# Expert token lists by 8-byte indirect transfers through DRAM, in place of one-hot matmuls

## The chip, the cores and the metric

The kernel runs on one core of a Trainium2 chip. The metric is the device time of one execution in microseconds (us), as the median of several runs. Before the change it is 3347.19 us (three runs, 3345.39 to 3347.9).

## What is computed

One layer of a diffusion backbone over 2048 tokens of width 1024: a mixer (convolution heads and neighbourhood attention), then expert-choice routed SwiGLU experts, then a final RMSNorm. The change lies in the experts. The reference, cut to them:

```python
def ec_moe(h, w_router, w_gate, w_up, w_down):
    B, T, _ = h.shape
    cap = EC_FACTOR * T // N_EXPERTS             # 2 * 2048 // 16 = 256
    aff = jax.nn.softmax((h @ w_router).astype(jnp.float32), axis=-1)
    wts, tok = lax.top_k(jnp.swapaxes(aff, 1, 2), cap)
    bidx = jnp.arange(B)[:, None, None]
    xs = h[bidx, tok]
    hid = jax.nn.silu(jnp.einsum('becd,edf->becf', xs, w_gate)) * jnp.einsum('becd,edf->becf', xs, w_up)
    y = jnp.einsum('becf,efd->becd', hid, w_down) * wts[..., None].astype(h.dtype)
    return jnp.zeros_like(h).at[bidx, tok].add(y)
```

Each of the 16 experts takes the 256 tokens that like it best. It needs their numbers (to gather their rows and to add the results back) and their weights.

## The kernel before, in words

The program runs in stages: input projection, convolution and attention, output projection with the router, routing, experts. The expert stage (`moe`, from L1140) takes the last two thirds of the time.

**Routing** (`route`, L1083). For every token and expert it leaves in `slot` (128 partitions x 16 token blocks x 16 experts) the token's place in the expert's list, 1 to 256, or 0 if the expert did not take it. `lg` holds the affinities. `vals` holds, per token and expert, five bf16 numbers: the block number, the partition, and the affinity in three pieces.

**The token list of an expert** (`prep`, L1168). For each of the 16 token blocks VectorE (DVE) compares a row 1 to 256 with the block's `slot` column, which gives a one-hot matrix `oh` (L1171). TensorE (PE) multiplies the 16 one-hot blocks, in two halves of 128 places, with `vals` (L1177 to L1178): 32 matmuls of 5 columns per expert. DVE turns the five sums into the token number `idx` and the weight `wt` (L1180 to L1185). Two indirect transfers on GpSimd's (POOL's) queue then gather the tokens' rows from DRAM into `xr` (L1191).

**The chunks.** An expert has 24 chunks in a list (L1208): 16 of gate/up (`gate_up`, L1228: 32 matmuls, 16 of 512 columns and 16 of 256) and 8 of down (`down`, L1255: 24 matmuls of 512 columns). For each chunk `load` (L1213) brings 1 MB of weights into `raw` (3 buffers) over SyncE's (SP's) queue; ScalarE (ACT) casts it to `whi` and DVE subtracts to give `wlo` (L207, L208; 3 buffers each). In the loop over chunks (L1379) the load of chunk i+2 is issued before the work of chunk i.

**What else is in the loop.** `prep(e+1)` is called at gate/up chunk 8 of expert e (L1384); `gather(e+1, part)` (L1195), which transposes the gathered rows on PE and splits them, at down chunks 1 to 4 of expert e; `finish(e)` (L1357) at its last chunk: DVE scales the result into `y` and POOL adds it to `acc` in DRAM with two indirect transfers (L1365). The last two experts take other paths (`rows_of`, `finish_late`, `last_part`, `final`).

**What sets the order.** The framework's scheduler orders each engine's instructions: among those that its own plan takes to be ready, the one written first goes first. So work written later is put into an engine's idle places as soon as the plan has its inputs. Within `tc.manual_schedule(engines=ENG)` (L1372, `ENG` is POOL) POOL's instructions keep the order in which they are written; the region ends at chunk `REG`, 3 before the change (L1397). `self.order(a, b)` (L201) puts a behind b on its engine; `PIN` uses it for the first one-hot block of expert 2. An engine runs its instructions in that order: one that waits holds up all behind it.

The lines that matter most:

```python
            for i, (s, e, f) in enumerate(chunks):
                if i:
                    load(i + 2)
                if s == "gu":
                    gate_up(i)
                    if f == PF and e + 1 < NE:
                        prep(e + 1)
```

Of the kernel before, what the change touches and what calls it, by code (L numbers as in the profile page):

```python
# [10 lines left out]
F32 = mybir.dt.float32  # L11
F32R = mybir.dt.float32r
BF16 = mybir.dt.bfloat16
F16 = mybir.dt.float16
I32 = mybir.dt.int32
AF = mybir.ActivationFunctionType
OP = mybir.AluOpType
# [3 lines left out]
P = 128  # L21
D = 1024
KT = D // P
T = 2048
NT = T // P
# [9 lines left out]
E = 16  # L35
NE = E
F = 2048
CAP = 256
# [7 lines left out]
CTX0 = ("q", 0)  # L46
ALL = {mybir.EngineType.DVE, mybir.EngineType.PE, mybir.EngineType.Activation, mybir.EngineType.Pool, mybir.EngineType.SP}
MAIN = {mybir.EngineType.DVE, mybir.EngineType.PE, mybir.EngineType.Activation}
REG = 3
PIN = (2,)  # L50
ENG = {mybir.EngineType.Pool}
LAT = 0.8
LEAD = 2.2
# [70 lines left out]
class Net:  # L124
# [1015 lines left out]
    def moe(self):  # L1140
        nc, tc, A, S = self.nc, self.tc, self.A, self.S
        with ExitStack() as es:
            pool = es.enter_context(tc.tile_pool(name="p6", bufs=1, reuse_waits="tile"))
            ps = es.enter_context(tc.tile_pool(name="ps6", bufs=1, space=PSUM, reuse_waits="tile"))
            g2 = pool.tile([P, D], F32, name="g2")
            X, XR, AXW = {}, {}, {}
# [19 lines left out]
                                                       op0=OP.mult, op1=OP.add)  # L1166

            def prep(e):  # L1168
                oh = pool.tile([P, NT, CAP], BF16, name="oh", bufs=1)
                for c in range(NT):  # L1170
                    m = nc.vector.tensor_scalar(oh[:, c, :], self.iob, self.slot[:, c, e:e + 1], None, op0=OP.is_equal)  # L1171
                    if e in PIN and c == 0:
                        self.order(m, self.xlo)
                pi = ps.tile([P, 2, 8], F32, name="tp6", tag="tp", bufs=1)
                for hf in range(2):
                    for c in range(NT):
                        nc.tensor.matmul(pi[:, hf, :5], oh[:, c, hf * P:(hf + 1) * P], self.vals[:, c, e, :],  # L1177
                                         start=(c == 0), stop=(c == NT - 1))  # L1178
                ax = pool.tile([P, 5, 8], F32, name="ax", bufs=2)[:, :2]
                nc.vector.tensor_copy(ax[:, :, :5], pi[:, :, :5])  # L1180
                idx = pool.tile([P, 2], I32, name="idx", bufs=3)
                wt = pool.tile([P, 2], F32, name="wt", bufs=3)
                nc.vector.scalar_tensor_tensor(idx, ax[:, :, 0], float(P), ax[:, :, 1], op0=OP.mult, op1=OP.add)
                nc.vector.tensor_add(wt, ax[:, :, 2], ax[:, :, 3])
                nc.vector.tensor_add(wt, wt, ax[:, :, 4])  # L1185
                AXW[e] = (idx, wt)
                XR[e] = []
                for i in range(2):
                    xr = pool.tile([P, D], F32, name="xr", bufs=2)
                    XR[e].append(xr)  # L1190
                    nc.gpsimd.indirect_dma_start(  # L1191
                        out=xr, out_offset=None, in_=S["h2d"][:, :],
                        in_offset=bass.IndirectOffsetOnAxis(ap=idx[:, i:i + 1], axis=0))

            def gather(e, part):  # L1195
                if part == 0:
                    X[e] = pool.tile([P, KT, 2 * CAP], F32R, name="xt6", bufs=2)
                xt = X[e]
                i, a = divmod(part, 2)
                xr = XR[e][i]  # L1200
                tp = ps.tile([P, 4, P], F32, name="tp6", tag="tp" if e else "mm", bufs=1 if e else 7)
                for k in range(4):
                    nc.tensor.transpose(tp[:, k, :], xr[:, (4 * a + k) * P:(4 * a + k + 1) * P], self.ident)
                hi = xt[:, 4 * a:4 * a + 4, i * P:(i + 1) * P]
                nc.scalar.copy(hi, tp)
                self.xlo = nc.vector.tensor_sub(xt[:, 4 * a:4 * a + 4, CAP + i * P:CAP + (i + 1) * P], tp, hi.bitcast(F32))  # L1206
# [6 lines left out]
            def load(i):  # L1213
                if i >= len(chunks):
                    return
                s, e, f = chunks[i]
                raw = pool.tile([P, 2, 1024], F32, name="raw", tag="raw", bufs=3)
                src = A["w_gu"][e, f].rearrange("p a k c -> p a (k c)") if s == "gu" else A["w_dn"][e, f]
                nc.sync.dma_start(raw, src)
                hi = pool.tile([P, 2, 1024], F32R, name="whi6", bufs=3)  # L1220
                lo = pool.tile([P, 2, 1024], F32R, name="wlo6", bufs=3)
                for a in range(2):
                    self.split(raw[:, a], hi[:, a], lo[:, a], nc.gpsimd if i < 3 else None)
                W[i] = (hi, lo)
# [3 lines left out]
            def gate_up(i):  # L1228
                s, e, f = chunks[i]
                hi, lo = [a.rearrange("p a (k c) -> p a k c", k=KT) for a in W.pop(i)]  # L1230
                xt = X[e]
                pg = []
                for a in range(2):
                    p_ = ps.tile([P, 512], F32, name="pgu", tag="mm", bufs=7)
                    for k in range(KT):
                        nc.tensor.matmul(p_, hi[:, a, k], xt[:, k, :], start=(k == 0), stop=False)  # L1236
                        nc.tensor.matmul(p_[:, :CAP], lo[:, a, k], xt[:, k, :CAP], start=False, stop=(k == KT - 1))  # L1237
                    pg.append(p_)
                t = pool.tile([P, 2, CAP], F32, name="gt6", bufs=2)
                for a in range(2):  # L1240
                    nc.scalar.copy(t[:, a], pg[a][:, CAP:])  # L1241
                    nc.vector.tensor_add(t[:, a], pg[a][:, :CAP], t[:, a])  # L1242
                sl = pool.tile([P, CAP], F32, name="sl6", bufs=2)
                nc.scalar.activation(sl, t[:, 0], AF.Silu)
                nc.vector.tensor_mul(sl, sl, t[:, 1])  # L1245
                hh = pool.tile([P, CAP], F32R, name="hh", bufs=20)
                hl = pool.tile([P, CAP], F32R, name="hl", bufs=20)
                self.split(sl, hh, hl)
                hid[e, f] = (hh, hl)
# [50 lines left out]

            def rows_of(e):
                idx = AXW[e][0]
                ga = pool.tile([P, 2, D], F32, name="ga", bufs=1)
                for a in range(2):
                    nc.gpsimd.indirect_dma_start(
                        out=ga[:, a], out_offset=None, in_=S["acc"][:, :],
                        in_offset=bass.IndirectOffsetOnAxis(ap=idx[:, a:a + 1], axis=0))
                return ga
# [48 lines left out]
            def finish(e):  # L1357
                idx, wt = AXW[e]
                for a in range(2):
                    y = pool.tile([P, D], F32, name="y6", tag="y6", bufs=2)  # L1360
                    for b in range(2):
                        sb = slice(b * 512, (b + 1) * 512)
                        nc.vector.scalar_tensor_tensor(y[:, sb], py[e][a][b], wt[:, a:a + 1], g2[:, sb],  # L1363
                                                       op0=OP.mult, op1=OP.mult)
                    nc.gpsimd.indirect_dma_start(  # L1365
                        out=S["acc"][:, :], out_offset=bass.IndirectOffsetOnAxis(ap=idx[:, a:a + 1], axis=0),
                        in_=y, in_offset=None, compute_op=OP.add)
# [8 lines left out]
            prep(0)  # L1376
            for i in range(4):
                gather(0, i)
            for i, (s, e, f) in enumerate(chunks):  # L1379
                if i:  # L1380
                    load(i + 2)
                if s == "gu":
                    gate_up(i)
                    if f == PF and e + 1 < NE:  # L1384
                        prep(e + 1)
                    if e == 0 and f in (3, 6, 9, 12, 15):
                        gate2(2 * f // 3 - 2)
                else:
                    if 0 <= f - GF < 4 and e + 1 < NE:
                        gather(e + 1, f - GF)  # L1390
                    down(i)
                    if f == 7:
                        if e < NE - 2:
                            finish(e)
                        elif e < NE - 1:
                            finish_late(e, ga)
                if i == REG:  # L1397
                    region.close()
                if e >= NE - 2:
                    if i % 24 == 1:  # L1400
                        ga = rows_of(e)
                        if e == NE - 2:
                            gf = pool.tile([P, D], F32, name="gf")
                            nc.sync.dma_start(gf, A["ngf"].to_broadcast([P, D]))
                    if i - 24 * (NE - 2) in FIN:
                        final(FIN.index(i - 24 * (NE - 2)))
# [28 lines left out]
```

## Time and profile before

| | |
|---|---|
| median of 3 runs | 3347.19 us (3345.39 to 3347.9) |
| the profiled execution, its own time | 3346.83 us |
| its span in the profile | 3345.0 us |
| mean granted clock of TensorE | 0.986 |
| PE, DVE, ACT, POOL busy | 97%, 70%, 50%, 12% of the span |
| mean transfer rate | 190 GB/s |

The times of the trace count from the start of the span. The profile's rows name the line of the code, the engine, and the operation as output <- inputs. PEld is PE's loading of weights, which overlaps its matmuls. The expert stage starts near 1130 us; expert e from 1 to 13 starts near 1282 + 137 (e - 1). A row of a timeline may merge several instructions of one kind (x10); its duration then runs from the first one's start to the last one's end.

### The profile page before, as it was taken

The page shows a single profiled execution, that of the slowest core. Times are in us where ns is not written, and L with a number is a line of the kernel's source. Part 1 is how long each engine was busy: PE and PEld are TensorE (multiplying, and loading weights), DVE is VectorE, ACT ScalarE, POOL GpSimd, SP SyncE. Part 2 cuts the span into 40 slices and gives each one's busy share as a digit, 9 for nine tenths or more (in the row PEclk, how much of TensorE's full clock was granted, in tenths as well). Part 3 has the DMA queues.
Part 4 walks back from the last instruction along what each step waited for, and adds up shares of the span by engine and source line. Part 5 has one row for each costly group of instructions (what it writes and reads, how often), then busy time and mean ns, then how long its engine had stood idle before and what let it go on. Part 6 is the DMA issues. An engine that isn't in the chain of part 4 may idle for free. (4 is left out here: it accounts for less than half of the span.)

```text
span 3345.0 us, 47917 instructions
## 1 busy us (share of the span) xinstructions
PE 3242.2 (97%) x18394; PEld 2749.2 (82%) x18394; DVE 2344.0 (70%) x3645; ACT 1660.1 (50%) x2788; POOL 414.1 (12%) x729
## 2 busy tenths in 40 slices
PE   7999999999999599999999999999999999999998
PEld 4788887899777488888888888888888888888887
DVE  6898988888666776665666756656667666665766
ACT  7211124788433255454554545545555455454654
POOL 3100002344211200000000000000000000001221
PEclk9999999999999699999999999999999999999999
DMA  6244329997432466565565565665556556556765
GB/s 234 76 139 127 110 98 249 227 224 189 146 127 107 170 220 197 201 204 198 202 208 191 206 201 191 212 201 195 196 201 207 197 201 200 195 210 208 283 251 202
DMA packets 159585, 635.61 MB, mean 190 GB/s; under 512 B 47926, under 2 KB 62678, under 8 KB 106108
## 3 DMA queue, kind: packets, MB, share of 16 engines
q1 hardware_dynamic: 138172, 542.68, 47.4%
q0 software_dynamic: 21184, 89.86, 10.9%
q8 instruction: 145, 2.38, 0.3%
q14 instruction: 84, 0.69, 0.1%
HBM read 560.38 MB, written 72.10 MB: 189 GB/s over the span
## 5 line engine op out<-in xcount | busy, mean ns | idle before, releaser
L1236 PE MATMUL pgu<-xt,whi 128*128 128x512 f32 x4096 | 1446.7, 398 | 0.5 <-DVE xt L1206 0.5
L208 DVE TENSOR_TENSOR wlo<-raw,whi 128x1024 fp32r<-128x1024 f32 x762 | 919.0, 1220 | 649.0 <-ACT whi L207 646.4
L1237 PE MATMUL pgu<-xt,wlo 128*128 128x256 f32 x4096 | 1149.8, 281 | 0.2 <-DVE wlo L208 0.2
L207 ACT CAST whi<-raw 128x1024 fp32r<-128x1024 f32 x768 | 793.1, 1050 | 565.7 <-PE py L1272 277.9
L1236 PEld LDWEIGHTS pgu<-xt,whi 128*128 128x128 f32 x4096 | 769.3, 188 | 189.8 <-DVE xt L1206 0.9
L1237 PEld LDWEIGHTS pgu<-xt,wlo 128*128 128x128 f32 x4096 | 773.7, 189 | 1.1 <-DVE wlo L208 0.5
L1268 PE MATMUL py<-whi,hh 128*128 128x512 f32 x1024 | 405.3, 396 | 0.0
L1269 PE MATMUL py<-wlo,hh 128*128 128x512 f32 x1024 | 399.8, 390 | 0.0
L1272 PE MATMUL py<-whi,hl 128*128 128x512 f32 x1024 | 316.4, 390 | 0.0
L534 DVE SCALAR_TENSOR_TENSOR cacc<-v,k,cacc 128x2048 f32<-128x2048 f32 x120 | 281.6, 2347 | 1.7
L1241 ACT COPY gt<-pgu 128x256 f32<-128x256 f32 x512 | 188.5, 368 | 177.2 <-PE pgu L1237 176.8
L471 PE MATMUL mm<-hhi,whi 128*128 128x512 f32 x576 | 227.1, 394 | 0.0
L1272 PEld LDWEIGHTS py<-whi,hl 128*128 128x128 f32 x1024 | 192.2, 188 | 41.5
L473 PE MATMUL mm<-hhi,wlo 128*128 128x512 f32 x576 | 224.5, 390 | 0.0
L1268 PEld LDWEIGHTS py<-whi,hh 128*128 128x128 f32 x1024 | 192.4, 188 | 39.0 <-issue 0.2
L472 PE MATMUL mm<-hlo,whi 128*128 128x512 f32 x576 | 224.2, 389 | 0.0
L1269 PEld LDWEIGHTS py<-wlo,hh 128*128 128x128 f32 x1024 | 192.5, 188 | 38.0 <-issue 0.2
L1242 DVE TENSOR_TENSOR gt<-pgu,gt 128x256 f32<-128x256 f32 x512 | 213.9, 418 | 6.0 <-ACT gt L1241 5.9
L207 ACT CAST hh<-sl 128x256 fp32r<-128x256 f32 x256 | 104.1, 406 | 223.2 <-DVE sl L1245 223.2
L1365 POOL DMA_INDIRECT acc<-y,idx x28 | 51.6, 1842 | 1263.8 <-DVE y L1363 1184.6
L737 DVE CUSTOM_DVE_ANT_0 pt<-sp,bi 128x640 f32<-128x640 f32 (+1 forms) x128 | 113.6, 887 | 31.0 <-PE sp L730 29.5
L208 DVE TENSOR_TENSOR hl<-sl,hh 128x256 fp32r<-128x256 f32 x256 | 108.8, 425 | 34.0 <-ACT hh L207 7.1
(317 smaller groups left out, 4122.8 us busy)
## 6 DMA issues: line engine op xcount, KB each, us to landing
raw<-w_gu SPq DMA_DIRECT2D x256, 1024.0 KB, 4.8
raw<-w_dn SPq DMA_DIRECT2D x128, 1024.0 KB, 4.8
bi<-bias SPq DMA_DIRECT2D x14, 960.0 KB, 11.0
wm<-wm POOLq DMA_DIRECT2D x24, 512.0 KB, 4.5
vb<-vd SPq DMA_DIRECT2D x119, 96.0 KB, 3.5
wraw<-w_in SPq DMA_DIRECT2D x20, 512.0 KB, 4.2
kh<-kh POOLq DMA_DIRECT2D x16, 576.0 KB, 12.5
kl<-kl POOLq DMA_DIRECT2D x16, 576.0 KB, 14.5
```

What stands on the lines that cost most here:

```text
L207: nc.scalar.copy(hi, full)
L208: (eng or nc.vector).tensor_sub(lo, full, hi.bitcast(F32))
L471: nc.tensor.matmul(ps, w[0][:, k, :], h[0][:, k, :], start=(k == 0), stop=False)
L472: nc.tensor.matmul(ps, w[0][:, k, :], h[1][:, k, :], start=False, stop=False)
L473: nc.tensor.matmul(ps, w[1][:, k, :], h[0][:, k, :], start=False, stop=(k == KT - 1))
L534: nc.vector.scalar_tensor_tensor(acc, v[:, w:w + T], cwt[:, j, w:w + 1], acc, op0=OP.mult, op1=OP.add)
L1236: nc.tensor.matmul(p_, hi[:, a, k], xt[:, k, :], start=(k == 0), stop=False)
L1237: nc.tensor.matmul(p_[:, :CAP], lo[:, a, k], xt[:, k, :CAP], start=False, stop=(k == KT - 1))
L1242: nc.vector.tensor_add(t[:, a], pg[a][:, :CAP], t[:, a])
L1268: nc.tensor.matmul(py[e][a][b], hh[:, sa], hi[:, ff, sb], start=(f == 0), stop=False)
L1269: nc.tensor.matmul(py[e][a][b], hh[:, sa], lo[:, ff, sb], start=False, stop=False)
L1272: nc.tensor.matmul(py[e][a][b], hl[:, sa], hi[:, ff, sb], start=False, stop=(f == 15))
```

## The change

For experts 2 to 15 (`NL = 2`) the one-hot matrices and their matmuls are gone; experts 0 and 1 keep them. `list_setup`, once, before the first chunk, makes on POOL and DVE two tables over all tokens and experts: an entry of 8 bytes (token number, affinity), and the row at which it is written: place - 1 for a token that the expert took, 256 + token number for one that it did not, so that each token has a row of its own. While expert e runs, POOL issues for expert e+2 16 indirect transfers (`list_put`, one before each of chunks 3 to 18), each of 128 entries to a DRAM tile of 2304 x 2 numbers that each expert has for itself; at chunk 21 one transfer reads the first 256 rows back (`list_get`). In `prep(e)` one DVE copy then takes the token numbers out as `idx`; the weights are used where they were read. The gather of the tokens' rows is unchanged (`fetch`).

`REG` becomes 335, so POOL keeps the written order up to the end of expert 13. `PIN` is gone; a copy in `list_setup` is put behind the last subtraction of expert 0's `gather`. `ga` now shares the buffer of `oh`.

```diff
-REG = 3
-PIN = (2,)
+REG = 24 * 14 - 1
+NL = 2
...
             def prep(e):
-                oh = pool.tile([P, NT, CAP], BF16, name="oh", bufs=1)
+                if e >= NL:
+                    nc.vector.tensor_copy(AXW[e][0], got.pop(e).bitcast(I32)[:, :, 0])
+                    fetch(e)
+                    return
+                oh = pool.tile([P, NT, CAP], BF16, name="oh", tag="oh", bufs=1)
                 for c in range(NT):
-                    m = nc.vector.tensor_scalar(oh[:, c, :], self.iob, self.slot[:, c, e:e + 1], None, op0=OP.is_equal)
-                    if e in PIN and c == 0:
-                        self.order(m, self.xlo)
+                    nc.vector.tensor_scalar(oh[:, c, :], self.iob, self.slot[:, c, e:e + 1], None, op0=OP.is_equal)
...
                 AXW[e] = (idx, wt)
+                fetch(e)
+
+            got = {}
+
+            def list_setup():
+                ids = pool.tile([P, NT * E], F32, name="ids")
+                nc.gpsimd.iota(ids, pattern=[[P, 2], [2 * P, NT // 2], [0, E]], base=CAP + 1, channel_multiplier=1,
+                               allow_small_or_imprecise_dtypes=True)
+                tv = pool.tile([P, NT, E, 2], F32, name="tv")
+                ent = tv.rearrange("p c e v -> p (c e) v")
+                nc.vector.tensor_scalar(ent[:, :, 0].bitcast(I32), ids, -(CAP + 1.0), None, op0=OP.add)
+                m = nc.vector.tensor_copy(ent[:, :, 1], self.lg.rearrange("p b s e -> p (b s e)"))
+                self.order(m, self.xlo)
+                sl = self.slot.rearrange("p c e -> p (c e)")
+                nc.vector.scalar_tensor_tensor(ids, sl, 0.0, ids, op0=OP.is_equal, op1=OP.mult)
+                row = pool.tile([P, NT, E], I32, name="row")
+                nc.vector.scalar_tensor_tensor(row.rearrange("p c e -> p (c e)"), ids, -1.0, sl, op0=OP.add, op1=OP.add)
+                return tv, row
+
+            def list_put(e, c):
+                tv, row = lists
+                if c == 0:
+                    S["lst", e] = tc.dram_tile([CAP + T, 2], F32, name=f"lst{e}")
+                nc.gpsimd.indirect_dma_start(
+                    out=S["lst", e][:, :], out_offset=bass.IndirectOffsetOnAxis(ap=row[:, c, e:e + 1], axis=0),
+                    in_=tv[:, c, e, :], in_offset=None)
+
+            def list_get(e):
+                t = pool.tile([P, 2, 2], F32, name="lst", bufs=3)
+                nc.gpsimd.dma_start(t, S["lst", e][:CAP].rearrange("(a p) v -> p a v", p=P))
+                AXW[e] = (pool.tile([P, 2], I32, name="idx", bufs=3), t[:, :, 1])
+                got[e] = t
+
+            def fetch(e):
+                idx = AXW[e][0]
                 XR[e] = []
...
-                ga = pool.tile([P, 2, D], F32, name="ga", bufs=1)
+                ga = pool.tile([P, 2, D], F32, name="ga", tag="oh", bufs=1)
...
+            lists = list_setup()
             for i, (s, e, f) in enumerate(chunks):
                 if i:
                     load(i + 2)
+                if NL <= e + 2 < NE:
+                    if 3 <= i % 24 < 3 + NT:
+                        list_put(e + 2, i % 24 - 3)
+                    elif i % 24 == 5 + NT:
+                        list_get(e + 2)
```

## Rows read from the trace of the kernel before

**Rows 1.** The page's first part: busy time and share of each engine.

```profile
PE 3242.2 (97%) x18394; PEld 2749.2 (82%) x18394; DVE 2344.0 (70%) x3645; ACT 1660.1 (50%) x2788; POOL 414.1 (12%) x729
```

**Rows 2.** Busy times by stretch: PE, PEld, DVE, ACT, POOL, granted clock, DMA share, GB/s.

```profile
1419.00:1556.00 137.00, 137.00 (x754) 116.89 (x754) 87.99 (x142) 72.32 (x116) 6.29 (x4) 1.00 0.59 200
```

**Rows 3.** PE's timeline around the prep of expert 3: start, duration, instruction.

```profile
1469.55 0.40 PE L1236 MATMUL pgu<-xt,whi 128*128 128x512 f32 x1
1469.79 0.28 PE L1237 MATMUL pgu<-xt,wlo 128*128 128x256 f32 x1
1469.91 0.99 PE L1177 MATMUL tp<-vals,oh 128*128 128x5 bf16 x32
1470.76 0.47 PE L1236 MATMUL pgu<-xt,whi 128*128 128x512 f32 x1
1471.08 0.28 PE L1237 MATMUL pgu<-xt,wlo 128*128 128x256 f32 x1
```

**Rows 4.** The tile `oh`, whole span: counts and durations in ns (min/median/max).

```profile
L1177 PEld LDWEIGHTS <-oh x512: 95/96/118, 1130.1 to 3110.3; 128*128 128x128 bf16 x171
L1177 PE MATMUL tp<-vals,oh x512: 165/165/189, 1130.1 to 3110.3; 128*128 128x5 bf16 x171
L1171 DVE TENSOR_SCALAR oh<-iob,slot x256: 273/281/365, 1129.8 to 2984.4; 128x256 bf16<-128x256 bf16 x128
```

**Rows 5.** DVE's timeline after that prep.

```profile
1475.47 2.05 DVE L1171 TENSOR_SCALAR oh<-iob,slot 128x256 bf16<-128x256 bf16 x10
```

**Rows 6.** POOL's timeline over four experts, with the idle time before and its releaser.

```profile
1282.44 1.64 POOL L1365 DMA_INDIRECT acc<-y,idx  x1 [137.42 <-DVE y L1363]
1289.58 2.07 POOL L1365 DMA_INDIRECT acc<-y,idx  x1 [5.50 <-issue]
1335.22 1.57 POOL L1191 DMA_INDIRECT xr<-h2d,idx  x1 [43.57 <-issue]
...
1419.35 1.61 POOL L1365 DMA_INDIRECT acc<-y,idx  x1 [80.81 <-DVE y L1363]
...
1556.38 1.61 POOL L1365 DMA_INDIRECT acc<-y,idx  x1 [80.89 <-DVE y L1363]
...
1692.41 1.63 POOL L1365 DMA_INDIRECT acc<-y,idx  x1 [80.05 <-DVE y L1363]
```

**Rows 7.** DMA issues on POOL's queue: count, size, median us from issue to landing.

```profile
acc<-y,idx POOLq DMA_INDIRECT x30, 6.6
...
out<-of,idx POOLq DMA_INDIRECT x4, 3.8
...
wm<-bm POOLq DMA_DIRECT2D x3, 4.0 KB, 1.8
```

**Rows 8.** Timelines of ACT and DVE at one chunk's weights.

```profile
1453.03 1.05 ACT L207 CAST whi<-raw 128x1024 fp32r<-128x1024 f32 x1 [0.76 <-PE pgu L1236]
...
1455.59 1.22 DVE L208 TENSOR_TENSOR wlo<-raw,whi 128x1024 fp32r<-128x1024 f32 x1
```

**Rows 9.** Groups of instructions, 1260 to 3060 us: busy, mean ns, idle before, releasers.

```profile
L207 ACT CAST whi<-raw 128x1024 fp32r<-128x1024 f32 x634 | 655.6, 1051 | 510.4 <-PE py L1272 253.9 <-PE pgu L1236 166.1 <-issue 90.4
```

**Rows 10.** The tile `raw`, 1300 to 3000 us: DVE's subtraction, ns (min/median/max).

```profile
L208 DVE TENSOR_TENSOR wlo<-raw,whi x598: 1211/1219/1227, 1300.2 to 2998.8; 128x1024 fp32r<-128x1024 f32 x200
```

**Rows 11.** POOL's and ACT's timelines at the end of expert 13.

```profile
3058.97 1.64 POOL L1365 DMA_INDIRECT acc<-y,idx  x1 [80.77 <-DVE y L1363]
3066.14 2.07 POOL L1365 DMA_INDIRECT acc<-y,idx  x1 [5.54 <-DMA acc<-y,idx]
...
3078.69 1.06 ACT L1288 ACTIVATE of<-xf 128x1024 f32<-128x1024 f32 x1 [5.27 <-DMA xf<-acc]
```

**Rows 12.** DVE's timeline at the end of routing and the start of expert 0.

```profile
1127.22 0.88 DVE L1127 SCALAR_TENSOR_TENSOR cum<-cum,of,mk 128x256 f32<-128x256 f32 x2
...
1138.64 2.64 DVE L1171 TENSOR_SCALAR oh<-iob,slot 128x256 bf16<-128x256 bf16 x13
...
1147.90 0.42 DVE L1242 TENSOR_TENSOR gt<-pgu,gt 128x256 f32<-128x256 f32 x1 [2.74 <-ACT gt L1241]
```

**Rows 13.** The page's third part: packets, MB, share of 16 engines.

```profile
q0 software_dynamic: 21184, 89.86, 10.9%
```

## The prediction

> **What bounds the kernel now.** I read the page first: PE is busy for 97% of the span, far above DVE and ACT [rows 1]. A mean over stages says little of one stage, so the second view is busy time by stretch: while expert 2 runs, PE is busy for 137.00 of 137.00 us at a granted clock of 1.00, that is 2.4 GHz, DVE for 88 and POOL for 6 [rows 2]. In this stage an instruction taken off PE's queue shortens the time by the room that it took there, and work taken off DVE gives nothing by itself. The third view is PE's timeline around one prep, for that room; the fourth POOL's timeline, since the new work goes there; the fifth the timelines of ACT and DVE, for how late DVE may be before PE notices.
>
> **What is removed from PE.** Fourteen experts lose their 32 small matmuls (512 now [rows 4], 64 after). Their price is a distance between starts, not a duration: 32 of them with 165 ns each would be 5.3 us, but they overlap. In the timeline a 256-column matmul starts at 1469.79; the next pair would start about 0.12 later, at 1469.91, and starts at 1470.76 because the block of 32 stands between: 0.85 us. The pair's second half then follows after 0.32 instead of 0.24 (1469.55 to 1469.79), another 0.08 [rows 3]. So 0.93 us per prep, and 14 x 0.93 = 13.0 us. I take all of it as gain, as PE has no idle time that it could vanish in [rows 2].
>
> The weight loads beside these matmuls last 96 ns each and their matmuls start 27 ns apart (0.85 / 32) [rows 3, 4]. The Trainium skill (TensorE: Matmul & The Clock Gate, LDWEIGHTS) gives a load's time as its columns over 1.2, in ns, an estimated 107 ns for 128; a prep of 32 loads in a row would then be 3.4 us and the gain 48 us, and the measured distance decides against it.
>
> **What is removed from DVE.** 14 x 16 comparisons of 0.28 us, about 0.2 apart in a run (2.05 for 10) [rows 4, 5], and three small operations per expert: some 50 us that lie beside PE. Worth nothing on the path. They had already been pulled an expert ahead: the run of ten stands right behind the prep before it [rows 5].
>
> **What is added at the start.** One iota on POOL and four DVE operations over 256 elements, at 0.44 each (0.88 for two [rows 12]) 1.8 us. They fall where 13 comparisons for expert 2 now take 2.64 us, and before a stretch in which DVE idles 2.74 us for the first products [rows 12]. Cost nothing; if that cover were gone, up to 1.8 us once.
>
> **What is added to POOL and the DMA engines.** Per expert 16 puts and one get. A put follows its predecessor into the same DRAM tile, as the two transfers into `acc` do: the second starts 7.14 us after the first, once that has landed [rows 6]. A put's spacing has no row. From above it is bounded by that pair, which moves 4 KB rows and adds: 7.1 us. From below by a transfer of 4 KB in all on this queue, which lands in 1.8 us [rows 7]. Nearest is the plain indirect write of 4 KB rows, landing in 3.8 us [rows 7]; with half a microsecond until the next starts (7.14 against 6.6 for the landing) I take 4.3 us. POOL's round per expert is then 9.2 us for the two adds (1282.44 to 1291.65), 16 x 4.3 = 69, about 3.2 for the two gathers (1.57 each [rows 6]) and some 4 for the get (twice the small transfer's 1.8 [rows 7]): 85 us, against 137 from one expert to the next (1282.44 to 1419.35 [rows 6]). Even 7.1 us gives 130. So POOL keeps up, `finish` finds it free, and the list is there an expert before its use. The gather of rows, written at chunk 8, is queued behind six puts: ready some 35 us into the expert (52 with 7.1), and needed at down chunk 1, 17/24 x 137 = 97 us in. That leaves 45 us or more to cover it.
>
> On the DMA engines a put is 128 tiny packets. If each cost as much as a mean packet of this queue does now (10.9% of 16 x 3345 us over 21184 packets, 0.28 us [rows 13]), a put would take 128 x 0.28 / 16 = 2.2 us of each engine, once per chunk of 5.7 us, on top of a share of 0.59 [rows 2]: 0.98 in sum, just below one, at a price per packet that one of 8 bytes should stay far under (that queue's mean is 89.86 MB / 21184 = 4.2 KB). ACT's casts wait for PE's buffers and not for the weights' landing [rows 9], so a somewhat slower load is hidden. DVE's subtraction takes 1211 to 1227 ns in all 598 cases, POOL's transfers beside it or not [rows 10]: no cost there.
>
> **The sum.** 13.0 us off. The profiled execution took 3346.83 us, 0.36 less than the median of 3347.19; from the median, 3334.2 us. Consecutive experts with the same work differ (1419.35 to 1556.38 is 137.0, on to 1692.41 is 136.0 [rows 6]), so I allow this case 5 us down and 6 up: 3329 to 3340.
>
> **Rival 1, slower: DVE stands still for the list.** The copy that takes `idx` out of the list waits for the get. DVE's order is the scheduler's, which fills DVE's idle places with later work as soon as its plan has the inputs; the comparisons show how far ahead that goes [rows 5]. Behind a copy put too early stand the subtractions that make `wlo`. How late may DVE be? ACT's cast starts when PE frees the oldest of three buffers, at 1453.0; PE then has two chunks of 5.7 us left, to 1464.4, and DVE is through with that chunk at 1456.8 [rows 8]: 7.6 us. So the rival decides once the 16 puts in a row take over 7.6 us more than planned, 0.48 per put. For it: at the end of expert 13 a load waits for two chained adds, and ACT's square, placed for it, held ACT up for 5.27 us [rows 11]: a plan short by up to 1.8 us for each of three transfers. Against it: small plain writes need not be misjudged as those were, and in steady state no DVE row waits for a transfer now. With 1.0 us per put PE loses 14 x (16 - 7.6) = 118 us and the time is 3347 + 118 - 13 = 3452; with 1.8, 14 x 21.2 = 297 us and 3631. Chance 0.22.
>
> **Rival 2, slower: the chain of puts outlasts the expert.** That needs a spacing over (137 - 9.2 - 3.2 - 4) / 16 = 7.5 us. With 8 us POOL falls 7.4 us behind per expert; the 40 us that the gathers have in hand last for five experts, the other eight pay: 59 us, 3393. Against it: the plain write of 512 times the bytes lands in 3.8 [rows 7]. Chance 0.06.
>
> A rule speaks for this rival: the Trainium skill (DMA: Bandwidth & Descriptors, Specifications) says that a transfer of less than 512 bytes makes the DMA engine read, modify and write. No run here has shown 8-byte writes to DRAM; if each put then cost what the reading and adding pair does, POOL's round would be 130 us, which still fits, and the sum would be the same.
>
> **Rival 3, no change: the gain is given back.** The same wait as in rival 1, but just past DVE's 7.6 us, by 0.4 to 1.4 us per expert, returns 6 to 20 us: 3341 to 3354. Chance 0.08.
>
> **How the numbers follow.** The forecast has 0.64. A measurement of this kernel can tell 0.2%, 6.7 us, from no change; the forecast and its own range (3329 to 3340) lie beyond that, so faster is 0.64, within 0.2% is rival 3 with 0.08, slower are rivals 1 and 2 with 0.28. To hold 8 in 10 the range goes from 3329 to 3400: it takes in the forecast, rival 3, rival 2 and the mild end of rival 1 (up to about 0.75 us per put). Faster and slower both have weight, so the likeliest case's own range stands beside it, as given.
>
> **What would show it.** Right: L1177 with 64 matmuls, experts 0.9 us shorter on PE, POOL with rows of puts 3 to 5 us apart and idle before each `finish`, DVE's copy without a wait. Rival 1: that copy, or the first `wlo` behind it, with idle time released by the get's landing, PE busy below 137 of 137, and PE waiting for `wlo`. Rival 2: POOL without idle time before the adds, and PE waiting for `xr`. The forecast is wrong if an expert keeps its 137 us although the 32 matmuls are gone.

## The result, and the profile after

The changed kernel takes **3850.04 us** (median of 4, 3842.7 to 3854.61) against 3346.42 for the kernel before beside it: a ratio of 1.1514 [1.1497, 1.1531], 504 us slower, where 3334.2 was forecast. The profiled execution took 3849.88 us, its span is 3848.0. It is rival 1, at a size beyond the dearer of the two prices given for it.

The page's first part of the kernel after, to be read against [rows 1]:

```profile
PE 3261.3 (85%) x17946; PEld 2762.1 (72%) x17946; DVE 2298.9 (60%) x3383; ACT 1637.9 (43%) x2788; POOL 662.9 (17%) x968
```

448 matmuls are gone from PE, and yet it is busy for 19 us more. POOL's work rose by 60% and reaches 17%: nothing is full any more. So something waits. The waits of PE, DVE and POOL in the kernel after (what waited and for what, us in total, times, longest):

```profile
PE pgu L1274 <- DVE wlo L208: 489.8, 14, 36.9
...
DVE idx L1170 <- DMA lst<-lst: 595.9, 13, 48.1
...
DVE idx L1170 <- issue: 46.7, 1, 46.7
...
POOL lst L1212 <- DMA lst<-tv,row: 833.5, 209, 9.0
```

Once per list, 14 times, DVE stands still for the list's read-back and PE for DVE. One of these stops on DVE's timeline, kernel after, expert 2 (start, duration, instruction, idle time before and its releaser):

```profile
1354.48 1.23 DVE L208 TENSOR_TENSOR wlo<-raw,whi 128x1024 fp32r<-128x1024 f32 x1 [1.73 <-ACT whi L207]
...
1355.95 1.22 DVE L208 TENSOR_TENSOR wlo<-raw,whi 128x1024 fp32r<-128x1024 f32 x1
...
1357.42 0.41 DVE L1279 TENSOR_TENSOR gt<-pgu,gt 128x256 f32<-128x256 f32 x1
1404.62 0.17 DVE L1170 COPY idx<-lst 128x2 int32<-128x2 int32 x1 [46.78 <-DMA lst<-lst]
1404.70 0.42 DVE L208 TENSOR_TENSOR hl<-sl,hh 128x256 fp32r<-128x256 f32 x1
1405.03 1.22 DVE L208 TENSOR_TENSOR wlo<-raw,whi 128x1024 fp32r<-128x1024 f32 x1
```

The same stop on PE's timeline:

```profile
1370.27 0.40 PE L1273 MATMUL pgu<-xt,whi 128*128 128x512 f32 x1
1406.31 0.58 PE L1274 MATMUL pgu<-xt,wlo 128*128 128x256 f32 x1 [35.64 <-DVE wlo L208]
1406.68 0.63 PE L1273 MATMUL pgu<-xt,whi 128*128 128x512 f32 x1
1407.11 0.41 PE L1274 MATMUL pgu<-xt,wlo 128*128 128x256 f32 x1
...
1411.08 0.40 PE L1273 MATMUL pgu<-xt,whi 128*128 128x512 f32 x1
1411.32 0.28 PE L1274 MATMUL pgu<-xt,wlo 128*128 128x256 f32 x1
```

A copy of 0.17 us, which nobody needs before the next expert, stands in DVE's queue ahead of the `wlo` that PE needs now. It waits 46.78 us; PE lives on finished weights for 11.14 of them and then loses 35.64. Afterwards PE is slow for a while: in a pair of matmuls (512 columns with `whi`, then 256 with `wlo`) the second follows the first after 0.43 us (1406.68 to 1407.11), and after 0.24 from 1411.08 on. What the copy waits for is on POOL's timeline, kernel after, the same expert:

```profile
1308.40 1.68 POOL L1402 DMA_INDIRECT acc<-y,idx  x1 [85.77 <-DVE y L1400]
1315.60 2.01 POOL L1402 DMA_INDIRECT acc<-y,idx  x1 [5.52 <-DMA acc<-y,idx]
1317.92 0.99 POOL L1212 DMA_INDIRECT lst<-tv,row  x1 [0.31 <-issue]
1327.34 0.97 POOL L1212 DMA_INDIRECT lst<-tv,row  x1 [8.43 <-DMA lst<-tv,row]
...
1393.71 0.95 POOL L1212 DMA_INDIRECT lst<-tv,row  x1 [2.58 <-DMA lst<-tv,row]
1397.30 0.95 POOL L1212 DMA_INDIRECT lst<-tv,row  x1 [2.63 <-DMA lst<-tv,row]
1402.23 0.75 POOL L1218 DMA_DIRECT2D lst<-lst  x1 [3.98 <-DMA lst<-tv,row]
1481.90 1.65 POOL L1402 DMA_INDIRECT acc<-y,idx  x1 [78.92 <-DVE y L1400]
```

The copy was DVE's next instruction at 1357.8, when only six of the 16 puts had been issued. That is 40 us after the first put (1317.92), and the list came 87 us after it. Read back from this place, the scheduler's plan had the list ready after some 40 us, if it let the chain begin where POOL did. The expert lasts 173.5 us (1308.40 to 1481.90) in place of 136.9 [rows 6], and POOL, with 79 us idle, is not what holds it.

Busy times by stretch, kernel after (columns as in [rows 2]): the end of the stop, the 4.6 us behind it, and what follows.

```profile
1400.00:1406.30 6.30, 0.00 (x0) 0.00 (x0) 1.68 (x4) 0.00 (x0) 0.75 (x1) 0.50 0.02 0
1406.31:1410.90 4.59, 4.59 (x14) 3.96 (x15) 3.60 (x6) 2.81 (x6) 0.00 (x0) 0.50 0.43 143
1411.08:1440.00 28.92, 28.92 (x164) 25.26 (x163) 22.93 (x38) 18.99 (x36) 0.00 (x0) 1.00 0.65 222
```

The clock is granted at 0.50 (1.2 GHz) at the end of PE's stop and for 4.6 us of full work behind it, then at 1.00 (2.4 GHz). There 14 matmuls take 4.59 us, 0.66 a pair, and later 164 take 28.92, 0.35 a pair: seven pairs cost 2 us more. **The account**: 489.8 of waiting + 14 x 2 of slow clock - 13 of removed matmuls, as forecast, = 505, against 504 measured.

### The profile page after: what moved, and what is told of

It is laid out like the page before. It is cut to its first block, busy times and chain, and to the rows that moved or that the text cites. A ratio compares the mean times of both kernels' runs of the same rounds, so it can differ in the third digit from the quotient of the medians.

```text
span 3848.0 us, 46997 instructions
## 1 busy us (share of the span) xinstructions
PE 3261.3 (85%) x17946; PEld 2762.1 (72%) x17946; DVE 2298.9 (60%) x3383; ACT 1637.9 (43%) x2788; POOL 662.9 (17%) x968
## 5 line engine op out<-in xcount | busy, mean ns | idle before, releaser
L1274 PE MATMUL pgu<-xt,wlo 128*128 128x256 f32 x4096 | 1165.6, 285 | 489.8 <-DVE wlo L208 489.8
L1273 PE MATMUL pgu<-xt,whi 128*128 128x512 f32 x4096 | 1470.8, 403 | 0.8 <-DVE xt L1243 0.8
L1274 PEld LDWEIGHTS pgu<-xt,wlo 128*128 128x128 f32 x4096 | 789.1, 193 | 494.9 <-DVE wlo L208 494.3
L1273 PEld LDWEIGHTS pgu<-xt,whi 128*128 128x128 f32 x4096 | 784.3, 191 | 193.9 <-DVE xt L1243 1.0
L1212 POOL DMA_INDIRECT lst<-tv,row x224 | 242.5, 1082 | 848.7 <-DMA lst<-tv,row 833.5
```

The source lines that it names most:

```text
L1212: nc.gpsimd.indirect_dma_start(out=S["lst", e][:, :], out_offset=bass.IndirectOffsetOnAxis(ap=row[:, c, e:e + 1], axis=0), in_=tv[:, c, e, ...
```

## The experiments

The theory, A: the copy's place in DVE's order is the whole loss; the transfers cost nothing. The rivals: B, the traffic of the puts or POOL's work costs time by itself; C, the chain of puts is too long for the expert; D, a list that is written earlier is ready in time.

**1. The copy in its written place** (`split` now returns its subtraction).

```diff
-                    nc.vector.tensor_copy(AXW[e][0], got.pop(e).bitcast(I32)[:, :, 0])
+                    m = nc.vector.tensor_copy(AXW[e][0], got.pop(e).bitcast(I32)[:, :, 0])
+                    self.order(m, self.hlo)
...
-                self.split(sl, hh, hl)
+                self.hlo = self.split(sl, hh, hl)
```

> The copy that takes the token numbers out of the list is put behind DVE's last subtraction of the chunk in which it is written (gate/up chunk 8 of the expert before its use); nothing else changes. Theory A, DVE's queue is held by a copy that stands too early: DVE no longer waits for the get, PE's 490 us of waits for the subtraction go, and 14 x 0.93 us of one-hot matmuls stay saved: 3333 us (3328 to 3340). Theory B, the chain of 16 puts is itself too long for an expert: the time stays at least 50 us above 3346 (3400 and more), with PE waiting for the gathered rows. Theory C, the new transfers slow the weights' loads: PE waits for casts or subtractions behind loads, above 3400 too.

3334.22 us (10 runs), ratio 0.9969 [0.9956, 0.9982]. One dependency takes the 504 us away, with every put, get and byte still there. (That this is the forecast's 3334.2 is in part luck: the kernel before took 3343.23 beside these runs, not 3347.19.) DVE's timeline of this kernel:

```profile
1474.07 0.43 DVE L208 TENSOR_TENSOR hl<-sl,hh 128x256 fp32r<-128x256 f32 x1
1474.41 0.16 DVE L1170 COPY idx<-lst 128x2 int32<-128x2 int32 x1
```

POOL's timeline of this kernel over one expert, and the start of a later one:

```profile
1418.85 1.65 POOL L1403 DMA_INDIRECT acc<-y,idx  x1 [7.65 <-DVE y L1401]
...
1428.39 0.99 POOL L1213 DMA_INDIRECT lst<-tv,row  x1 [0.30 <-issue]
1436.91 1.82 POOL L1213 DMA_INDIRECT lst<-tv,row  x1 [7.53 <-DMA lst<-tv,row]
...
1546.18 0.75 POOL L1219 DMA_DIRECT2D lst<-lst  x1 [4.64 <-DMA lst<-tv,row]
1554.82 1.64 POOL L1403 DMA_INDIRECT acc<-y,idx  x1 [7.89 <-DVE y L1401]
...
1826.75 1.65 POOL L1403 DMA_INDIRECT acc<-y,idx  x1 [0.75 <-DVE y L1401]
```

The copy no longer waits. The experts follow each other every 135.97 us (1418.85 to 1554.82). The chain, no longer helped by stops, takes 118 us from the first put to the get (1428.39 to 1546.18), 7.05 us per put in the median: POOL has 7.89 us left in this expert and 0.75 in the tightest. Rival C did not happen, but it is that near.

**2. No copy**: the two columns of the list are handed to the transfers as they are (`Col` is a class that slices the list).

```diff
-                    nc.vector.tensor_copy(AXW[e][0], got.pop(e).bitcast(I32)[:, :, 0])
+                    got.pop(e)
...
-                AXW[e] = (pool.tile([P, 2], I32, name="idx", bufs=3), t[:, :, 1])
+                AXW[e] = (Col(t.bitcast(I32)), t[:, :, 1])
```

> No copy at all: the gathers and scatters take their token numbers straight from the list as it was read back, so no DVE instruction waits for the get before the expert's end. Theory A: as with the pinned copy, 3333 us (3328 to 3340), within 2 us of it. Theory B and C: 3400 and more, as with the pinned copy.

3332.43 us (12 runs), 0.9969 [0.9957, 0.9982], experts every 136.0 us. Nothing on DVE waits for the list, and the time is that of the pinned copy. Two unlike edits, each of the one instruction alone, agree: A.

**3. The list one expert earlier**, the copy free as in the kernel after.

```diff
-NL = 2
+NL = 3
...
-                if NL <= e + 2 < NE:
+                if NL <= e + 3 < NE:
```

The list's and `idx`'s buffers rise from 3 to 4.

> The list is written and read back three experts ahead instead of two (experts 0 to 2 keep the one-hot), the copy is left to the scheduler as in the changed kernel. Theory A: the copy follows its get in the plan wherever that stands, so 13 stalls of some 36 us stay: 3800 to 3830 us. Theory D, the list is simply read back too late for its use: an expert more of lead cures it, about 3335 us.

3772.69 us (one run). DVE's timeline of this kernel at one of its stops:

```profile
1704.89 0.17 DVE L1170 COPY idx<-lst 128x2 int32<-128x2 int32 x1 [47.59 <-DMA lst<-lst]
```

And PE's timeline:

```profile
1706.58 0.58 PE L1274 MATMUL pgu<-xt,wlo 128*128 128x256 f32 x1 [36.76 <-DVE wlo L208]
```

The copy moves forward with the list and waits as long as before. The time falls below A's 3800 to 3830 by about 30 us, for a smaller sum of stops (420 us of PE's waits for `wlo`; the first of the 13 copies doesn't wait and the second only 28.20 us), but comes nowhere near D. Distance doesn't help against an order that is filled as soon as the plan allows.

**4 and 5. The lists written and read, but the one-hot matrices used**: the transfers alone. In the second of the two, `ga` has its own buffer again.

```diff
-                if e >= NL:
-                    nc.vector.tensor_copy(AXW[e][0], got.pop(e).bitcast(I32)[:, :, 0])
-                    fetch(e)
-                    return
...
-                AXW[e] = (pool.tile([P, 2], I32, name="idx", bufs=3), t[:, :, 1])
```

> All experts take their token numbers from the one-hot matmuls as before; the lists are written and read back all the same, and nobody uses them. Theory A: the transfers alone cost nothing, 3346 us (3340 to 3352). Theory B and C: POOL's chain or the traffic alone costs a good part of the 504 us, 3400 and more.

3364.16 us (6 runs), 1.006 [1.0043, 1.0077]: a miss, 20 us over. The excess is in one place, PE's waits of this kernel from expert 0 on:

```profile
PE tp L1235 <- DMA xr<-h2d,idx: 10.5, 1, 10.5
PE tp L1175 <- DVE oh L1171: 5.5, 2, 5.3
```

Both lie between 3180 and 3201, where the one-hot matrices of expert 15 come due; they share a buffer with `ga`. (The changed kernel has no such matrices there.) So the second version:

> As the run with unread lists, but ga has its own buffer again, as before the change. That run was 0.6% slower than before and its trace shows the loss in one place, expert 14, where the one-hot of expert 15 waits for the buffer that ga holds. Theory A (the transfers themselves cost PE nothing): without the sharing 3343 us (3336 to 3350), the kernel before. Theory C (the traffic costs some 20 us spread over the experts): it stays at 3357 to 3367.

3343.85 us (11 runs), 0.9997 [0.9985, 1.0009]. The puts, the gets, POOL's fixed order and the tables cost nothing that can be measured. B falls.

**6 and 7. POOL's written order ended after the start** (`REG` 3), with the puts of a list freed from each other, and without.

```diff
-REG = 24 * 14 - 1
+REG = 3
...
+                for q in puts[e]:
+                    tc.declare_no_dep(m.ins, q.ins, reason="rows differ")
+                puts[e].append(m)
```

> The puts of one list no longer wait for each other (the dependency between them is taken away, their rows differ; POOL's fixed order ends at chunk 3 again, which that needs); the copy is left to the scheduler as in the changed kernel. Theory A1, the lateness is made by 16 landings in a row that the plan takes for shorter: without the chain 16 issues of 1.0 to 1.6 us and one landing remain, DVE is late by less than the 10 us that PE does not notice, and the time is near 3335 us (3328 to 3360). Theory A2, it is POOL's issuing that the plan misjudges: stalls stay, above 3500 us.

3517.9 us (4 runs), 1.0508 [1.0489, 1.0527].

> The changed kernel with POOL's fixed order ended at chunk 3, as before the change; puts chained, copy left to the scheduler. Theory A: the place of the copy in DVE's queue, not POOL's order, makes the loss: 3800 to 3900 us. Theory F, the fixed order of POOL's queue holds the get back behind other transfers: near 3340 us.

3568.7 us (one run). Neither tells what it was made for: the first is slow as A2 has it, but not for A2's reason, and the second lies near neither of its forecasts. With POOL's order left to the scheduler all 224 puts are issued in one burst, 1141 to 1473 in the first and 1139 to 1519 in the second, and the copies, pulled forward with them, stop DVE mostly for another reason, the third buffer of `idx`. DVE's waits from expert 0 on, of the second kernel:

```profile
DVE idx L1170 <- DMA acc<-y,idx: 208.3, 10, 148.6
DVE idx L1170 <- DMA lst<-lst: 81.0, 1, 81.0
```

In the first row a copy waits until an earlier expert has added its result and so given an `idx` back; in the second the first copy waits for its list, as in the kernel after. PE loses 137.53 us behind the longest of the one and 76.27 behind the other. In the first kernel, with the puts freed, the first copy waits only 15.0 us for its list, and PE loses 155.31 us behind the buffer. The puts have another place, and it is still the copy that costs.

**8 and 9. The dose**: the copy behind the `wlo` that DVE makes while chunk 18, or chunk 22, of the expert that writes the list runs. That is the `wlo` of two chunks later; `LO` keeps the subtractions. The edit for chunk 18:

```diff
+                    self.order(m, LO[24 * (e - 2) + 18 + 2])
```

> The copy is put behind the subtraction of the weights that is done while chunk 18 runs, of the expert in which the list is written: some 106 us into it. With the pinned copy's trace the list is there some 136 us in, a little sooner when the weights' loads pause: DVE waits 20 to 30 us. Theory A with a reserve of 10.7 us (DVE waits 47, PE loses 36 in the changed kernel): PE loses 9 to 19 us in each of 14 experts, 3334 + 130 to 270 = 3460 to 3600 us, and in every expert DVE's wait less PE's loss is again 10 to 12 us. If the loss came from anything other than DVE's wait: 3334 or 3850.

3513.34 us, 1.0506 [1.049, 1.0522]. The time is as forecast, the reserve isn't. DVE's timeline of this kernel at one stop:

```profile
1404.66 0.17 DVE L1170 COPY idx<-lst 128x2 int32<-128x2 int32 x1 [15.81 <-DMA lst<-lst]
```

And PE's timeline:

```profile
1407.78 1.12 PE L1241 MATMUL tp<-ident,xr 128*128 128x128 f32 x4 [11.19 <-DVE xt L1244]
```

PE loses 11.19 of 15.81 us: 4.6 in hand, not 11, because in the down chunks PE doesn't run out of `wlo` first but of the buffer of its transposes, which DVE empties (`xt`).

> As the run with the copy behind the weights of chunk 18, but behind those of chunk 22, some 23 us later and past the transposes of the next expert's rows. There DVE waited 15 us and PE lost 10, so the copy here meets a list that is there or nearly: DVE waits 0 to 6 us. Theory A (PE notices DVE's lateness only past a reserve of some microseconds): no loss, 3334 us (3328 to 3345). Without a reserve, each of 14 waits would count: up to 3334 + 84 = 3418.

3336.84 us (10 runs), 0.9977 [0.9964, 0.9989]; DVE waits for the list only 13.5 us in 4 cases (5.3 at most) and PE not at all. The same instruction waits for the same list, and its cost is set by where it stands: 36, 11 or 0 us per expert.

**10. The puts freed from each other, in POOL's written order, the copy free**; a one-column memset on POOL stands between two puts.

```diff
+                for q in puts[e]:
+                    tc.declare_no_dep(m.ins, q.ins, reason="rows differ")
+                puts[e].append(m)
+                nc.gpsimd.memset(pad, 0.0)
```

> Within POOL's fixed order the puts of one list no longer wait for each other (dependency taken away, a one-column fill of POOL between them); the copy is left to the scheduler as in the changed kernel. If the lateness is made by the landings in a row (7.0 us from put to put with the weights' loads beside them, 2.3 at most in the plan), DVE's wait falls from 47 us to below 25 and the time below 3560 us, perhaps to 3334; if not, some 47 us and 3850 stay.

3497.0 us, 1.046 [1.0443, 1.0477]: below the 3560 us that stood for landings in a row, and far above 3334. POOL's timeline of this kernel over one list:

```profile
1442.28 0.99 POOL L1213 DMA_INDIRECT lst<-tv,row  x1 [0.31 <-issue]
1443.26 0.12 POOL L1221 MEMSET pad<- 128x1 f32 x1
1443.57 0.96 POOL L1213 DMA_INDIRECT lst<-tv,row  x1 [0.18 <-issue]
...
1473.82 0.75 POOL L1225 DMA_DIRECT2D lst<-lst  x1 [3.51 <-DMA lst<-tv,row]
```

DVE's timeline behind it:

```profile
1476.36 0.17 DVE L1170 COPY idx<-lst 128x2 int32<-128x2 int32 x1 [22.45 <-DMA lst<-lst]
```

And PE's:

```profile
1478.04 0.58 PE L1281 MATMUL pgu<-xt,wlo 128*128 128x256 f32 x1 [11.31 <-DVE wlo L208]
```

The list is done in 32 us in place of 84 to 118, and still the copy waits 22.45 us, since it has moved forward with it: it was DVE's next instruction 11.6 us after the first put. PE has the same 11.14 us in hand (22.45 - 11.31). Freeing the puts thus halves the wait (46.78 to 22.45 us), and the plan is early even where no put waits for another: 16 issues of 0.96 alone are 15.4 us, more than 11.6. Whether it has the puts begin too early, at the two adds ahead of them, or prices each too low, no run here separates.

**11. Both: no copy, and the puts freed.**

> Both: no copy, and puts that do not wait for each other. POOL's round of 16 puts and a get falls from 131 us to below 60, but PE is the bound with or without that: 3332 us, within 4 us of the run without the copy. If POOL's nearly full round cost PE something there, 5 us or more faster.

3328.71 us (6 runs), 0.9952 [0.9937, 0.9968]: the fastest, and faster than both kernels of the change. Its interval overlaps that of experiment 2, and its experts follow every 135.9 us in place of 136.0, so that freeing the puts is not shown to be worth anything on the clock; but POOL is through with a list after 40 us.

## Why the prediction was wrong

**What failed is the wait of DVE's copy**. The forecast had "DVE's copy without a wait"; it waited some 47 us per expert, and PE lost 489.8 us in all. The text saw this as rival 1, and **rival 1's price and chance** failed in the step "a plan short by up to 1.8 us for each of three transfers". The wait was 46.78 us over 16 puts, 2.9 per put, where 1.0 and 1.8 were priced. The rival's formula was good: 14 x (46.8 - 7.6) = 549, so 3883, against 3850.04. The evidence [rows 11] was a load behind two adds, and it was carried over to 16 puts without the question that mattered: what does the plan take a put for? The text sized the real spacing at 4.3 and gave the plan's no figure. The kernel after gives one, which the text could not have: the whole list at 40 us, at most 2.3 for each of 17 transfers if the plan let the chain begin where POOL did. Beside that, even the text's 4.3 would be 2.0 us late per put, four times the 0.48 from which the rival decides, and rival 1 the likeliest case. Without a figure for the plan, a chance of 0.22 had little under it.

**The spacing** was too small: 7.05 us beside the weights' loads (experiment 1) where 4.3 was taken; the upper bound, 7.1, was the value. "Nearest is the plain indirect write" went by the kind of transfer. The bound that had the right company, two transfers chained on this queue while the weights stream in, was the better neighbour. Rival 2 was therefore not the 0.06 of a far case: its threshold was 7.5 us, and POOL's idle time fell to 0.75 us in one expert.

A rule stood beside that rival: the Trainium skill (DMA: Bandwidth & Descriptors, Specifications) has writes below 512 bytes read, modified and written back. The runs neither show nor exclude it: the same 8-byte puts follow each other at 7.05 us beside the loads and at 3.59 in a stop of the kernel after (1393.71 to 1397.30), where nothing else moves. Half of the spacing is thus the company they are in, whatever their size does to the rest.

**DVE's reserve** of 7.6 us was right as a count and too small as an allowance for a wait: that is 11.14 us in gate/up, in two kernels. In the stop shown DVE's last `wlo` was done at 1357.17 and PE through with its chunk at 1370.67, 13.5 later; less the chunk's own 5.7, DVE was 7.8 us ahead, as counted. But PE first needs only the first of a chunk's two `wlo`, which is done about 1.5 earlier, and an estimated 1.9 of the wait fall where DVE would have idled anyway (the 1.73 before 1354.48, a chunk earlier). At the transposes the allowance is 4.6, so it isn't a constant of the kernel.

**Not foreseen**: the slow clock behind each stop, 14 x 2 us.

**Right**: the removed matmuls. Experiments 1 and 2 gain 0.31% [0.18, 0.44], some 10 us (6 to 15), with 13.0 forecast. By the periods the pinned kernel has a mean of 136.0 per expert (135.8 to 136.2), and the kernel before 136.9 or 137.0 in nine of the 13 (POOL's timeline; the first of them in [rows 6]): the 0.93 us of [rows 3] is there in these. The other four have 136.0 to 136.2 before, too, at shorter pairs behind the prep (a mean of 0.348 us in place of 0.354), and gain next to nothing; why they were faster, no run shows. By the rule of the Trainium skill (TensorE: Matmul & The Clock Gate, LDWEIGHTS) that the prediction weighed, with the loads one after the other, it would have been an estimated 48; the runs are with the distance between starts. **Right** as well that the tables, POOL's work and the transfers cost nothing (experiment 5), and, with the copy in its place (experiments 1 and 2), that PE waits for no list and, from expert 1 on, for no gather. And right was what rival 1 would look like: idle time before the copy "released by the get's landing", and "PE waiting for `wlo`", are the waits shown above.

## What to carry to other kernels

Before a result is taken through a chain of dependent transfers, ask of its first reader not when it is needed but where the scheduler will put it: an engine runs in order, and a cheap reader that is planned too early stops everything behind it for the whole error of the plan, here 16 puts' worth. Price the chain twice, by the trace and by what the order already shows of the plan, and look at the difference. Then pin that reader where the result is surely there, or remove it, as here by handing the transfer the column that the copy would have made; a longer lead or a faster chain alone doesn't cure it.

## What the runs showed of the hardware

Puts of 128 entries of 8 bytes lengthen the weights' loads beside them far more than they weigh. Queues (packets, MB, share of 16 engines) and issues (count, KB each, median us to landing) over one expert, first the kernel before, expert 2 (1419 to 1556):

```profile
q1 hardware_dynamic: 3452, 25.13, 51.6%
q0 software_dynamic: 576, 2.10, 7.3%
...
raw<-w_gu SPq DMA_DIRECT2D x16, 1024.0 KB, 4.8
```

and then the kernel of experiment 1, 1418.85 to 1554.82:

```profile
q1 hardware_dynamic: 3454, 25.15, 76.3%
q0 software_dynamic: 1120, 2.12, 7.7%
...
raw<-w_gu SPq DMA_DIRECT2D x16, 1024.0 KB, 7.8
...
lst<-tv,row POOLq DMA_INDIRECT x16, 6.2
```

The 16 puts and the get are 544 packet records (1120 - 576), so 32 for each and not the 128 per put that the prediction counted, and raise their own queue's share by 0.4 points. The weights' queue, with the same bytes, goes from 51.6% to 76.3%, and a load of 1 MB lands in 7.8 us in place of 4.8, longer than a chunk of 5.7. It is the transfers that do this: experiment 5, which has all one-hot matmuls as well, shows 71.9% and 7.8 us (1416.17 to 1553.08). PE sees none of it here (experiment 5: 0.9997 of the time before); the loads are issued two chunks ahead, and the DMA engines are busy for 0.85 of the time in place of 0.59 (1419 to 1556), so not full. What such puts cost where loads are the bound, no run shows.

The other way round the weights lengthen the puts. In the stop of the kernel after, 1382 to 1402, nothing but puts moves (busy times by stretch):

```profile
1382.00:1402.00 20.00, 0.00 (x0) 0.00 (x0) 0.00 (x0) 0.00 (x0) 4.76 (x5) 0.50 0.01 0
```

and a put lands in a median of 3.3 us there, against 6.2 above (issues, the same stretch):

```profile
lst<-tv,row POOLq DMA_INDIRECT x5, 3.3
```
